# A two-layer SSD, window-attention and hyena encoder on one core: decay rows stored a second time, hyena forward transform by residues, key and value columns moved ahead

## The chip, the cores and the metric

The kernel runs on one core of one Trainium2 chip, in a single launch. The core's engines are TensorE (PE, matmuls, with PEld for its weight loads), VectorE (DVE), ScalarE (ACT), GpSimd (POOL) and SyncE (SP); each works through its own list of instructions in order and waits on semaphores for the others and for DMAs. The metric is the device time of one execution in microseconds (us), as the median of several runs. Lower is better.

## The reference

Two sequences (256 tokens "prompt", 512 tokens "sample") go with the same weights through two encoder layers of width 2048, all in float32. A layer is

```python
h = rms_norm(x, norm_g)
u = h @ w_in
z, xbc, dt_raw, q, k, v, g_att, hy_proj, g_hy = split(u)
y_ssd = ssd_branch(z, xbc, dt_raw, ...)      # width 1024
y_att = attention_branch(q, k, v, g_att, ...)  # width 512
y_hy = hyena_branch(hy_proj, g_hy, ...)      # width 512
x = x + concat([y_ssd, y_att, y_hy]) @ w_out
```

The state-space branch runs a scan in chunks of 128 tokens, forward and backward, for 16 heads of 64 channels: inside a chunk with a matrix of decays, and between chunks with a state that is multiplied into the output together with the exponent of the cumulative decay:

```python
lmat = exp(where(tril, a_cs[..., :, None] - a_cs[..., None, :], -inf))
y_diag = einsum('bcgels,bcsgep->bclgep', cb[:, :, :, None] * lmat, xdt)
y_off = einsum('bclgn,bcgepn,bcgel->bclgep', cm, prev, exp(a_cs))
```

The hyena branch multiplies spectra: `u = xb*v`, `y = irfft(rfft(u, 2L) * rfft(kern))[:L]`, `y = xa*(y + u*d)`. The attention looks at a window of 128 tokens to either side, with 8 query heads and 2 key/value heads. Each branch's output is multiplied by a SiLU gate and normalised.

## The kernel before

All 768 tokens (512 + 256, `T`) are held in channels-by-tokens layout. `OPH` and `OPL` are the high and low part of the layer's input operand in fp32r, a format in which a float32 product is made of three matmuls: high x high, high x low, low x high. The projection weights come in columns of 128 outputs, `W(0)` to `W(45)` per layer and then `w_out`. `gemm` (L141 is the matmul helper in the profile) computes one column: four loads of raw weights on SP's queue, eight splits of a weight tile (`split_w`: `hi` on ACT, then `lo` on DVE), and 16 k-tiles x 2 halves of the tokens x 3 products = 96 matmuls of 128x384 into the banks `gs` (tokens 0 to 383) and `gq` (384 to 767). One split serves 12 matmuls. The tiles of splits are few (a ring), so ACT may run only a little ahead of PE. All helpers that record an ACT, DVE or PE operation have the lines L138, L128/L135 and L141.

The order of the work is the program's own. Besides the columns there are generators, held by an object `Background`: after each quarter of a column `bg.step()` lets each of them run on to its next `yield`, so that its matmuls stand between those of the column, and its ACT and DVE work between splits. `bg.later(n, f)` runs `f` n steps later, `bg.mid` holds work that is run at the middle of the next quarter (`bg.half()`), and `bg.flush(g)` runs the rest of a generator at once. Generators' matmuls write PSUM tiles named `m` (four buffers); their SBUF tiles are `t` (pool `t2`, 16 buffers of 128x512) and `s` (pool `s3`, 14 buffers of 128x768).

In each layer the columns come in this order: W0 to W3 (the scan's B and C), the step sizes `dt` (`gemm_dt`), W4 to W11 (the scan's input, turned and stored in `XS(j)`), W12 to W19 (hyena's xb and v), W20 to W27 (the scan's gate z), W28 to W31 (hyena's xa), W32 (K), W33 (V), W34 to W37 (q), W38 to W41 and W42 to W45 (the gates of hyena and attention), then the 16 columns of `w_out`.

Three generators matter here.

- `ssd_gen` computes the cumulative decays `adt` summed along the chunk, turns them into rows, and stores them in DRAM as `rows_d` (L638). Then it works on eight pairs of heads (`pair`), each in some nine steps, with a new pair started while the last one is in its sixth. A pair loads its rows broadcast over the 128 partitions in three parts `R0`, `R1`, `R2` (`rows`, L684, two loads of 256 KB each), makes of each a decay matrix (`prep`: DVE subtracts, ACT takes Exp), then the chunk states, then the output of the states `Y`. For the last it needs the rows a second time in another layout, with head 0 on partitions 0 to 63 and head 1 on 64 to 127, four chunks in each direction: these are the decay rows `E2` (L726, four loads per pair). ACT takes their Exp (L750), DVE multiplies by `Y`. After the in-chunk matmuls (L758) come the six sums that write `XS(j)` (L760 to L767).

```python
src = rows_d[l, d, h0:h0 + 2, cs[i]:cs[i] + n, :]
load(out=t[:, i:i + n, :], in_=bass.AP(src.tensor, src.offset,
     [[NCH * 128, 2], [0, 64], [128, n], [1, 128]]))
```

- `hyena_gen` runs twice per layer (each for 256 channels, `hy[0]` and `hy[1]`). It turns its input into even and odd time points (`to_time`), and makes the forward transform by matmuls with a table (`forward`, L515): for the long sequence 24 matmuls of 128x256 at each of two calls, for 2 x 128 frequencies. `product` multiplies by the filter's spectrum; then the products and the inverse table are split into high and low part, and 48 inverse matmuls follow. The consumer of `W(28 + j)` flushes `hy[j // 2]` before it uses the result.
- `filter_gen` makes the filter spectra `kd` of the next layer with the same forward tables.

After the scan's gate the sum of squares goes through `rms`: PE's sums over partitions, ACT's square root, and `scale_ssd`, in which DVE scales the eight tiles of `XS` and POOL's queue stores them to `ys_d` (L1037). The attention's tiles then take the place of `XS`: `new_xs(F32R)` after the four `xa` columns gives out the same memory for K's high half `KH`, which the consumer of W32 writes with four ACT copies of 64x768 (L138, `XS<-s`), and for the queries. Every DMA but the weights' is issued on POOL's queue (a POOL instruction stands in line behind all before it); the weights' are on SP's.

Of the kernel before, what the change touches and what calls it, by code (L numbers as in the profile page):

```python
# [97 lines left out]
def trunk(ctx: ExitStack, tc: tile.TileContext, xT, w_in, w_dt, w_out, prm, brow, w1, mlpv, w2, w3, w4,  # L98
# [83 lines left out]
    rows_d = drp.tile([DEPTH, 2, 16, NCH, 128], F32, name="rows_d")  # L182
    ys_d = drp.tile([DEPTH, 8, 128, T], F32, name="ys_d")
# [215 lines left out]
    def filter_gen(l):  # L399
# [7 lines left out]
        for half in range(2):  # L407
            hc = slice(256 * half, 256 * half + 256)
            for pm in (1, 0):
# [40 lines left out]
                def freq_part(f, G, nk, L, slot):  # L450
# [11 lines left out]
                    if pm == 0:  # L462
                        STT(kk[:, 1], p[:, 0], 1.0 / L, kk[:, 1], MUL, SUB)
                    else:
                        STT(kk[:, 1], p[:, 0], -1.0 / L, kk[:, 1], MUL, ADD)
# [18 lines left out]
    def hyena_gen(l, half, us, ys):  # L484
# [9 lines left out]
        srcs = (((0, 256), (256, 512), (1, 256)), ((257, 512), (p0, p1), (p0 + 1, p1)))  # L494
        U = [[r3(), r3()] for _ in range(2)]

        def to_time(j):
            for b in range(2):
                p = mp((128, 3, 128))
                for i, (a, e) in enumerate(srcs[b]):  # L500
                    nc.tensor.transpose(p[:, i, :], us[j][:, a:e:2], ident)
                split(p, *(x[:, :, 128 * j:128 * j + 128] for x in U[b]))
# [12 lines left out]
        def forward(fs, ev, odd):  # L515
# [16 lines left out]
            TT(B[:, 1, :], cs[:, 1, :], pn[:, 0, :], SUB)  # L532
            return A, B

        def product(A, B, slot):
# [12 lines left out]
            TT(y[:, 0, :], B[:, 0, :], B[:, 1, :], SUB)  # L548
            TT(y[:, 1, :], B[:, 0, :], B[:, 1, :], ADD)
# [13 lines left out]
        AB = forward(fS, (0, 1), (2, 3))  # L563
        yield
        yield
# [38 lines left out]
    def ssd_gen(l, dtT, BT, CT, ready):  # L604
# [24 lines left out]
        yield  # L629
        for b in range(3):  # L630
# [25 lines left out]

        FW, BW = (0, 1, 2, 4), (1, 2, 3, 5)
# [16 lines left out]
        def pair(j, bt, cbF, cbB):  # L674
# [599 lines left out]
```

## Time and profile before

| | |
|---|---|
| median of 3 runs | 2487.45 us (2485.87 to 2487.83) |
| the profiled execution | 2489.0 us |
| its span in the trace | 2487.2 us |
| mean granted TensorE clock | 0.993 |
| PE busy | 2441.4 us, 98% |
| DVE, ACT, POOL busy | 64%, 44%, 14% |
| chain that ended last | PE 90%, DMA 4%, issue 2% |
| DMA | 266.22 MB, mean 107 GB/s |

The span runs from the first to the last instruction in the trace; the execution's own time is 1.8 us longer. "Busy" counts the time in which an engine has at least one instruction at work. A matmul's duration in the trace includes the time it overlaps its neighbours, so sums of durations on PE are larger than the time they take. The granted clock is the share of full speed that the chip gave TensorE in a stretch.

### The profile page before, as it was taken

The page shows a single profiled execution, that of the slowest core. Times are in us where ns is not written, and L with a number is a line of the kernel's source. Part 1 is how long each engine was busy: PE and PEld are TensorE (multiplying, and loading weights), DVE is VectorE, ACT ScalarE, POOL GpSimd, SP SyncE. Part 2 cuts the span into 40 slices and gives each one's busy share as a digit, 9 for nine tenths or more (in the row PEclk, how much of TensorE's full clock was granted, in tenths as well). Part 3 has the DMA queues.
Part 4 walks back from the last instruction along what each step waited for, and adds up shares of the span by engine and source line. Part 5 has one row for each costly group of instructions (what it writes and reads, how often), then busy time and mean ns, then how long its engine had stood idle before and what let it go on. Part 6 is the DMA issues. An engine that isn't in the chain of part 4 may idle for free.

```text
span 2487.2 us, 40924 instructions
## 1 busy us (share of the span) xinstructions
PE 2441.4 (98%) x15066; PEld 2393.2 (96%) x15066; DVE 1580.5 (64%) x3410; ACT 1087.5 (44%) x2560; POOL 341.4 (14%) x683
## 2 busy tenths in 40 slices
PE   8999999999999999999999999999999999999998
PEld 7999999999999999999999999999999999999997
DVE  6888775558856766544476787766746477573333
ACT  6467653334334444333353575633332355352332
POOL 2033221221100010121200332201001000000001
PEclk9999999999999999999999999999999999999999
DMA  4266542443421132344421555423213111332223
GB/s 169 63 153 146 142 129 86 129 133 124 140 78 60 51 100 80 112 149 132 146 96 55 141 149 149 135 85 106 94 60 128 63 54 47 106 109 89 77 82 132
DMA packets 126921, 266.22 MB, mean 107 GB/s; under 512 B 30175, under 2 KB 36666, under 8 KB 126720
## 3 DMA queue, kind: packets, MB, share of 16 engines
q1 hardware_dynamic: 78048, 136.35, 17.7%
q0 software_dynamic: 48672, 127.26, 17.2%
q8 instruction: 118, 1.93, 0.3%
q14 instruction: 83, 0.68, 0.1%
HBM read 231.23 MB, written 34.18 MB: 107 GB/s over the span
## 4 chain that ended last, share of the span: by engine, by line
PE 90%; DMA 4%; issue 2%; DVE 1%; ACT 1%; POOL 1%; DVEq 0%; ACTq 0%; POOLq 0%
PE gs L141 38%; PE gq L141 38%; PE m L141 12%; DMA t<-rows_d 3%; PE m L848 1%; PE gl L141 1%; POOL t L726 0%; ACT t L138 0%; DMA XS<-in_xT 0%; DMA s<-in_xT 0%; ACT hi L138 0%; DVE lo L128 0%; DVE t L135 0%; PE m L1000 0%; DVE t L128 0%
## 5 line engine op out<-in xcount | busy, mean ns | idle before, releaser
L138 ACT ACTIVATE hi<-raw 128x256 fp32r<-128x256 f32 x984 | 405.6, 414 | 1040.1 <-PE gq L141 920.5
L128 DVE TENSOR_TENSOR lo<-raw,hi 128x256 fp32r<-128x256 f32 x984 | 412.5, 421 | 597.9 <-ACT hi L138 587.0
L141 PE MATMUL gs<-OPH,hi 128*128 128x384 f32 x1920 | 657.4, 342 | 18.1 <-ACT OPH L138 11.0
L141 PE MATMUL gs<-OPH,lo 128*128 128x384 f32 x1920 | 645.0, 336 | 0.6 <-DVE lo L128 0.5
L141 PE MATMUL gq<-OPH,lo 128*128 128x384 f32 x1920 | 644.4, 336 | 0.0
L141 PE MATMUL gs<-OPL,hi 128*128 128x384 f32 x1920 | 644.0, 336 | 0.1
L141 PE MATMUL gq<-OPH,hi 128*128 128x384 f32 x1920 | 644.1, 335 | 0.0
L141 PE MATMUL gq<-OPL,hi 128*128 128x384 f32 x1920 | 643.3, 335 | 0.0
L141 PEld LDWEIGHTS gs<-OPH,hi 128*128 128x128 f32 x1920 | 362.4, 189 | 25.2 <-ACT OPH L138 11.3
L141 PEld LDWEIGHTS gs<-OPH,lo 128*128 128x128 f32 x1920 | 361.6, 188 | 2.7 <-DVE lo L128 2.7
L141 PEld LDWEIGHTS gs<-OPL,hi 128*128 128x128 f32 x1920 | 362.3, 189 | 0.8 <-DVE OPL L135 0.6
L141 PEld LDWEIGHTS gq<-OPH,hi 128*128 128x128 f32 x1920 | 361.8, 188 | 0.0
L141 PEld LDWEIGHTS gq<-OPL,hi 128*128 128x128 f32 x1920 | 361.6, 188 | 0.0
L141 PEld LDWEIGHTS gq<-OPH,lo 128*128 128x128 f32 x1920 | 361.5, 188 | 0.0
L128 DVE TENSOR_TENSOR t<-t,t 128x512 f32<-128x512 f32 (+3 forms) x260 | 169.1, 668 | 26.5 <-ACT t L138 23.6
L135 DVE SCALAR_TENSOR_TENSOR s<-cv,prm_t,s 128x770 f32<-128x770 f32 x144 | 145.9, 1015 | 22.6 <-ACT s L138 21.9
L138 ACT ACTIVATE t<-s,dt 128x128 f32<-128x128 f32 x384 | 133.6, 391 | 18.9 <-DVE t L135 18.5
L128 DVE TENSOR_TENSOR s<-s,s 128x768 f32<-128x768 f32 (+2 forms) x126 | 112.8, 904 | 27.3 <-ACT s L138 26.7
L138 ACT ACTIVATE t<-t 128x512 fp32r<-128x512 f32 (+3 forms) x132 | 77.3, 587 | 92.4 <-DMA t<-rows_d 48.6
L128 DVE TENSOR_TENSOR t<-m,t 128x256 f32<-128x256 f32 (+3 forms) x157 | 72.3, 485 | 18.3 <-PE m L141 5.8
L684 POOL DMA_DIRECT2D t<-rows_d x96 | 68.8, 719 | 103.9 <-DVE XS L128 38.0
L138 ACT ACTIVATE t<-t,acs 128x128 f32<-128x128 f32 x192 | 73.6, 389 | 13.6 <-DVE t L135 13.6
(225 smaller groups left out, 2572.6 us busy)
## 6 DMA issues: line engine op xcount, KB each, us to landing
raw<-in_w_in SPq DMA_DIRECT2D x368, 256.0 KB, 3.0
raw<-in_w_out SPq DMA_DIRECT2D x128, 256.0 KB, 3.0
t<-rows_d POOLq DMA_DIRECT2D x96, 256.0 KB, 6.4
s<-in_xT POOLq DMA_DIRECT2D x24, 384.0 KB, 4.4
xs_d<-s POOLq DMA_DIRECT2D x16, 385.0 KB, 4.2
s<-xs_d POOLq DMA_DIRECT2D x16, 385.0 KB, 9.3
t<-rows_d POOLq DMA_DIRECT2D x32, 192.0 KB, 10.5
t<-in_decay POOLq DMA_DIRECT2D x24, 256.0 KB, 4.9
```

The source lines that it names most:

```text
L128: (eng or nc.vector).tensor_tensor(out=o, in0=a, in1=b, op=op)
L135: (eng or nc.vector).scalar_tensor_tensor(out=o, in0=a, scalar=s, in1=b, op0=op0, op1=op1)
L138: nc.scalar.activation(o, i, f, **kw)
L141: nc.tensor.matmul(o, lhsT=l, rhs=r, start=start, stop=stop)
L684: load(out=t, in_=rows_d[l, d, h0:h0 + 2, 2 * u:2 * u + 2, :].partition_broadcast(128))
L848: nc.tensor.transpose(pt[g][:, 128 * kb:128 * kb + 128], s[g][:, 128 * kb:128 * kb + 128], ident)
```

## The change

Three things change, and some lines with them.

1. **A second copy of the decay rows.** `ssd_gen` stores the rows it turns, besides into `rows_d`, also into a new DRAM tensor `ed_d`, in which each head has the four chunks that `E2` wants side by side (six further small stores a layer). `E2` is loaded from there: four loads per pair as before, but each fills 64 partitions with 512 elements of one head. The six sums at a pair's end become a function that runs at the middle of the next quarter column.
2. **Residues.** The time points of the long sequence are taken in the order 0, 2, 1, 3 modulo 4 instead of even, odd, and the frequencies of the tables in an order that pairs each with its mirror. `residues` then makes two transforms of 12 matmuls each, whose sums and differences (`sets`) give all frequencies; the second load of the forward table goes. The inverse table is loaded by `iv_load`, a step or more ahead of its splits.
3. **K and V first.** W32 (K) and W33 (V) come before the four `xa` columns W28 to W31; `new_xs` moves into K's consumer.

```diff
+    ed_d = drp.tile([DEPTH, 2, 16, 4, 128], F32, name="ed_d")
...
-        srcs = (((0, 256), (256, 512), (1, 256)), ((257, 512), (p0, p1), (p0 + 1, p1)))
+        srcs = (((0, SL, 4), (2, SL, 4), (1, SL, 4)), ((3, SL, 4), (p0, p1, 2), (p0 + 1, p1, 2)))
...
+        def residues(fs, a, tts):
+            ps = [mp((128, 2, 256)) for _ in range(2)]
+            for p, (fh, fl), tt in zip(ps, fs, tts):
+                uh, ul = um(tt)
+                for c in range(2):
+                    for n, (x, y) in enumerate(((fh, uh), (fh, ul), (fl, uh))):
+                        MM(p[:, c, :], x[:, a + c, :], y, n == 0, n == 2)
+            s = t2((128, 2, 256))
+            nc.scalar.copy(out=s, in_=ps[1])
+            E, F = t2((128, 2, 256)), t2((128, 2, 256))
+            TT(E, ps[0], s, ADD)
+            TT(F, ps[0], s, SUB)
+            return E, F
+
+        def sets(E, G, turned):
+            A, B = t2((128, 2, 256)), t2((128, 2, 256))
+            if turned:
+                TT(A[:, 0], E[:, 0], G[:, 1], ADD)
...
+            else:
+                for o, c in ((A, 0), (B, 1)):
+                    TT(o[:, 0], E[:, c], G[:, c], ADD)
+                    TT(o[:, 1], E[:, c], G[:, c], SUB)
             return A, B
...
-        AB = forward(fS, (0, 1), (2, 3))
-        yield
+        E, F = residues(fS, 0, (0, 1))
+        yield
+        G, H = residues(fS, 2, (2, 3))
         yield
...
-        spec = [[split(x, r2(), r2()) for x in product(*AB, 0)]]
-        yield
-        fS = freq(fwS[1], 2)
-        yield
-        yield
-        AB = forward(fS, (0, 1), (2, 3))
-        yield
-        spec.append([split(x, r2(), r2()) for x in product(*AB, 1)])
-        pss = [mp((128, 2, 256)) for _ in range(2)]
-        for eo in range(2):
-            iv = []
+        def iv_load(eo):
+            g = []
             for i in range(2):
                 f = t2((128, 2, 256))
                 load(out=f, in_=ivS[i, :, 2 * eo:2 * eo + 2, :])
-                iv.append(split(f, r3()[:, 0:2], r3()[:, 0:2]))
+                g.append(f)
+            return g
+
+        spec = [[split(x, r2(), r2()) for x in product(*sets(E, G, False), 0)]]
+        g = iv_load(0)
+        yield
+        yield
+        spec.append([split(x, r2(), r2()) for x in product(*sets(F, H, True), 1)])
+        pss = [mp((128, 2, 256)) for _ in range(2)]
+        for eo in range(2):
+            iv = [split(f, r3()[:, 0:2], r3()[:, 0:2]) for f in g]
+            if eo == 0:
+                yield
+                g = iv_load(1)
             yield
             yield
...
+        FW, BW = (0, 1, 2, 4), (1, 2, 3, 5)
...
             for d in range(2):
-                load(out=rows_d[l, d, :, 2 * b:2 * b + 2, :],
-                     in_=r.rearrange("h (c d) t -> h d c t", d=2)[:, d])
+                v = r.rearrange("h (c d) t -> h d c t", d=2)[:, d]
+                load(out=rows_d[l, d, :, 2 * b:2 * b + 2, :], in_=v)
+                cs = [(i, c - 2 * b) for i, c in enumerate((BW, FW)[d]) if c // 2 == b]
+                i, c = cs[0]
+                load(out=ed_d[l, d, :, i:i + len(cs), :], in_=v[:, c:c + len(cs)])
...
-            for d, cs in ((0, BW), (1, FW)):
+            for d in range(2):
                 t = t2((128, 4, 128))
-                for i, n in ((0, 3), (3, 1)):
-                    src = rows_d[l, d, h0:h0 + 2, cs[i]:cs[i] + n, :]
-                    load(out=t[:, i:i + n, :], in_=bass.AP(src.tensor, src.offset,
-                         [[NCH * 128, 2], [0, 64], [128, n], [1, 128]]))
+                for hh in range(2):
+                    load(out=t[64 * hh:64 * hh + 64], in_=ed_d[l, d, h0 + hh].partition_broadcast(64))
                 E2.append(t)
...
-            yield
-            dsk = P(l, PDS, j)
...
+            def final():
+                dsk = P(l, PDS, j)
...
+            bg.mid.append(final)
             yield
...
-        for j in range(4):
-            def f(ps, pq):
-                bg.flush(hy[j // 2])
...
-        new_xs(F32R)
-        KH = [XS(6), XS(7)]
-        kL = s3p.tile([128, T], F32R, tag="s3", name="kL")
-        KL = [(kL[:, 0:SL], kL[:, SL:T]), (t2((128, SL), F32R), t2((128, PL), F32R))]
+        KH, KL = [], []
 
         def f(ps, pq):
+            new_xs(F32R)
+            KH.extend((XS(6), XS(7)))
+            kL = s3p.tile([128, T], F32R, tag="s3", name="kL")
+            KL.extend(((kL[:, 0:SL], kL[:, SL:T]), (t2((128, SL), F32R), t2((128, PL), F32R))))
...
         gemm_col(W(33), f)
+        for j in range(4):
+            def f(ps, pq):
+                bg.flush(hy[j // 2])
+                a = hconv(j, ps, pq)
...
+            gemm_col(W(28 + j), f)
```

The constant tables (`constants`) get the new order of time points and frequencies, and a few signs in `forward`, `product` and `filter_gen` follow from it; their sizes stay.

**How the instructions move.** On POOL's queue in layer 0, at the second pair of heads (`rows_d` are the stored rows, `t` the tiles they are loaded into, `xs_d` the scan's input stored by a column's consumer, `h_d` a store of the filter generator), before:

```order
L375 DMA h_d<-s_1643 128x768
L746 DMA s_1714<-xs_d 128x770
L684 DMA t_1832<-rows_d 128x2x256
L684 DMA t_1834<-rows_d 128x2x256
L684 DMA t_1915<-rows_d 128x2x256
L684 DMA t_1917<-rows_d 128x2x256
L726 DMA t_1919<-rows_d 128x1x384
L726 DMA t_1919<-rows_d 128x1x128
L726 DMA t_1922<-rows_d 128x1x384
L726 DMA t_1922<-rows_d 128x1x128
```

and with the change:

```order
L716 DMA t_1839<-rows_d 128x2x256
L776 DMA s_1721<-xs_d 128x770
L716 DMA t_1841<-rows_d 128x2x256
L716 DMA t_1922<-rows_d 128x2x256
L716 DMA t_1924<-rows_d 128x2x256
L757 DMA t_1926<-ed_d 64x512 x2
L757 DMA t_1929<-ed_d 64x512 x2
L118 MEMSET cv 128x2 x3
L376 DMA h_d<-s_1650 128x768
```

The four `E2` loads, each of 384 or 128 elements on 128 partitions, are now two and two of 512 on 64; the store of `h_d`, which stood ahead of the row loads, now follows them.

On ACT in layer 0, from the square roots of the scan's norm on (`hi<-raw` is a weight split, `r` hyena's splits of its turned input, `XS<-s` the write of K's high half), before:

```order
L138 ACT_TABLE_LOAD
L138 ACTIVATE s_6712<-m,eps_93 128x512
L138 ACTIVATE hi<-raw 128x256
L138 ACTIVATE s_6712<-m,eps_93 128x256
L138 ACTIVATE r_6900<-m 128x3x128
L138 ACTIVATE hi<-raw 128x256 x2
L138 ACTIVATE r_6900<-m 128x3x128
L138 ACTIVATE hi<-raw 128x256 x5
L138 ACTIVATE r_6902<-m 128x3x128 x2
L138 ACTIVATE hi<-raw 128x256
L138 ACTIVATE s_6929<-cv,prm_t 128x770
```

and with the change:

```order
L138 ACT_TABLE_LOAD
L138 ACTIVATE s_6715<-m,eps_93 128x512
L138 ACTIVATE s_6715<-m,eps_93 128x256
L138 ACTIVATE r_6809<-m 128x3x128 x2
L138 ACTIVATE hi<-raw 128x256 x7
L138 ACTIVATE r_6811<-m 128x3x128 x2
L138 ACTIVATE hi<-raw 128x256
L138 ACTIVATE XS<-s_6929 64x768 x3
L138 ACTIVATE hi<-raw 128x256
L138 ACTIVATE XS<-s_6929 64x768
```

The K writes now follow eight weight splits after the square roots, with a ninth split ahead of the last of the four; before, they stood in the column after the four `xa` columns, of which the last row here (`s` from `cv`) is the first one's convolution. By the built program the first K write waits for the stores to `ys_d`.

## Rows read from the trace of the kernel before

**Rows 1.** The page, busy time: engine, us, share of the span, instructions.

```profile
PE 2441.4 (98%) x15066; PEld 2393.2 (96%) x15066; DVE 1580.5 (64%) x3410; ACT 1087.5 (44%) x2560; POOL 341.4 (14%) x683
```

**Rows 2.** Stretches: window, length, busy us of PE PEld DVE ACT POOL, PEclk, DMA, GB/s.

```profile
187.40:193.40 6.00, 3.94 (x14) 3.37 (x13) 5.97 (x13) 6.00 (x20) 0.00 (x0) 0.72 0.13 44
271.40:282.40 11.00, 7.00 (x33) 6.73 (x32) 6.02 (x15) 5.53 (x14) 0.72 (x1) 0.69 0.28 83
353.40:355.60 2.20, 0.76 (x10) 0.43 (x6) 0.41 (x2) 1.37 (x4) 1.09 (x2) 1.00 0.13 28
690.70:701.90 11.20, 6.61 (x29) 5.99 (x29) 10.10 (x22) 5.25 (x9) 2.37 (x10) 0.70 0.26 75
1521.60:1531.60 10.00, 6.09 (x34) 5.82 (x33) 4.96 (x13) 4.45 (x11) 0.72 (x1) 0.83 0.27 80
1602.40:1609.90 7.50, 5.47 (x29) 5.07 (x26) 2.99 (x10) 5.77 (x19) 1.33 (x5) 0.77 0.40 121
...
2301.00:2363.00 62.00, 62.00 (x360) 62.00 (x359) 20.52 (x42) 19.24 (x38) 1.07 (x2) 1.00 0.24 77
```

**Rows 3.** PE's waits: waiting group, releaser, us in all, cases, longest.

```profile
PE m L141 <- DVE XS L135: 7.9, 2, 4.0
```

**Rows 4.** ACT's timeline, 325 to 356 us: start, us each, what, and its wait before.

```profile
328.95 0.64 ACT L138 ACTIVATE t<-t 128x512 f32<-128x512 f32 x1 [2.67 <-DMA t<-rows_d]
...
350.64 0.63 ACT L138 ACTIVATE t<-t 128x512 f32<-128x512 f32 x1 [4.22 <-DMA t<-rows_d]
...
354.23 0.63 ACT L138 ACTIVATE t<-t 128x512 f32<-128x512 f32 x1 [2.96 <-DMA t<-rows_d]
```

**Rows 5.** Line L726: its issues (ns min/median/max), who waits, the landings.

```profile
L726 POOL DMA_DIRECT2D t<-rows_d x64: 797/817/855, 132.7 to 1595.3; - x64
...
  ACT t L138: 48.6, 24
...
DMA to landing us min/median/max: 5.9/10.3/13.7
```

**Rows 6.** Line L684, the rows' loads: issue to landing.

```profile
DMA to landing us min/median/max: 3.5/6.4/8.4
```

**Rows 7.** DMA queues, 350 to 353 us, then 341 to 343 us.

```profile
q0 software_dynamic: 33, 0.12, 11.2%
...
q0 software_dynamic: 101, 0.33, 71.8%
```

**Rows 8.** PE's groups by form: busy us, mean ns, idle before.

```profile
L141 PE MATMUL m<-r,t 128*128 128x256 f32 x432 | 59.8, 291 | 4.6 <-ACT r L138 4.6
```

**Rows 9.** PE's timeline, 618 to 626 and 689 to 705 us.

```profile
619.57 5.59 PE L141 MATMUL m<-r,t 128*128 128x256 f32 x46
...
695.61 8.94 PE L141 MATMUL m<-r,t 128*128 128x256 f32 x48 [4.58 <-ACT r L138]
```

**Rows 10.** Line L412, loads of 64 rows of weights: issue and landing.

```profile
L412 POOL DMA_DIRECT2D t<-in_w x16: 528/539/559, 354.1 to 1203.5; - x16
...
DMA to landing us min/median/max: 2.1/2.7/9.8
```

**Rows 11.** POOL's timeline, 1365 to 1377 us.

```profile
1370.73 2.51 POOL L638 DMA_DIRECT2D rows_d<-t  x5 [0.92 <-issue]
...
1374.89 0.73 POOL L684 DMA_DIRECT2D t<-rows_d  x1 [0.92 <-DMA rows_d<-t]
```

**Rows 12.** DVE's timeline, 1376 to 1384 us.

```profile
1379.71 1.14 DVE L135 SCALAR_TENSOR_TENSOR t<-t,acs,t 128x128 f32<-128x128 f32 x4 [3.52 <-DMA t<-rows_d]
```

**Rows 13.** ACT's timeline, 628 to 632 us.

```profile
630.39 0.46 ACT L138 ACTIVATE s<-m,eps 128x256 f32<-128x256 f32 x1
```

**Rows 14.** POOL's timeline, 625 to 655 us.

```profile
646.05 0.54 POOL L1037 DMA_DIRECT2D ys_d<-XS  x1 [0.67 <-PE gq L141]
```

**Rows 15.** Line L1037, the stores of `ys_d`: issue to landing.

```profile
DMA to landing us min/median/max: 3.3/4.8/7.1
```

**Rows 16.** ACT's groups by form: busy us, mean ns, idle before.

```profile
L138 ACT ACTIVATE XS<-s 64x768 fp32r<-64x768 f32 x24 | 20.3, 844 | 3.9 <-DVE s L135 2.9 <-DVE s L128 0.7
```

More of the change, by code (lines that the diff above doesn't have):

```diff
@@ L499, in to_time @@
                 p = mp((128, 3, 128))
-                for i, (a, e) in enumerate(srcs[b]):
-                    nc.tensor.transpose(p[:, i, :], us[j][:, a:e:2], ident)
+                for i, (a, e, n) in enumerate(srcs[b]):
+                    nc.tensor.transpose(p[:, i, :], us[j][:, a:e:n], ident)
                 split(p, *(x[:, :, 128 * j:128 * j + 128] for x in U[b]))
@@ L531, in forward @@
             TT(B[:, 0, :], pn[:, 0, :], cs[:, 1, :], ADD)
-            TT(B[:, 1, :], cs[:, 1, :], pn[:, 0, :], SUB)
+            TT(B[:, 1, :], pn[:, 0, :], cs[:, 1, :], SUB)
+            return A, B
+        def residues(fs, a, tts):
[15 more added lines that the diff above has]
+                TT(A[:, 0], E[:, 0], G[:, 1], ADD)
+                TT(A[:, 1], E[:, 0], G[:, 1], SUB)
+                TT(B[:, 0], G[:, 0], E[:, 1], SUB)
+                STT(B[:, 1], G[:, 0], -1.0, E[:, 1], MUL, SUB)
+            else:
+                for o, c in ((A, 0), (B, 1)):
+                    TT(o[:, 0], E[:, c], G[:, c], ADD)
+                    TT(o[:, 1], E[:, c], G[:, c], SUB)
             return A, B
@@ L547, in product @@
             TT(x[:, 1, :], A[:, 0, :], A[:, 1, :], SUB)
-            TT(y[:, 0, :], B[:, 0, :], B[:, 1, :], SUB)
-            TT(y[:, 1, :], B[:, 0, :], B[:, 1, :], ADD)
+            TT(y[:, 0, :], B[:, 0, :], B[:, 1, :], ADD)
+            TT(y[:, 1, :], B[:, 0, :], B[:, 1, :], SUB)
             return x, y
@@ L655, in ssd_gen @@
         yield
-        FW, BW = (0, 1, 2, 4), (1, 2, 3, 5)
         def group(g):
@@ L758, in pair @@
                     MM(o, X[:, c, hh, :], Ms[c // 2][:, hh, c % 2, :])
-            yield
-            dsk = P(l, PDS, j)
-            yT = Xf.rearrange("p (c t) -> p c t", c=NCH)
-            STT(yT[:, 0:4], t[:, 0:SL].rearrange("p (c t) -> p c t", c=4), dsk, yS, MUL, ADD)
-            STT(yT[:, 4:6], t[:, SL + GAP:T + GAP].rearrange("p (c t) -> p c t", c=2), dsk, yP, MUL, ADD)
-            for d, cs in ((0, BW), (1, FW)):
-                for i, n in ((0, 3), (3, 1)):
-                    c = cs[i]
-                    TT(yT[:, c:c + n], yT[:, c:c + n], E2[d][:, i:i + n], ADD)
+            def final():
+                dsk = P(l, PDS, j)
+                yT = Xf.rearrange("p (c t) -> p c t", c=NCH)
+                STT(yT[:, 0:4], t[:, 0:SL].rearrange("p (c t) -> p c t", c=4), dsk, yS, MUL, ADD)
+                STT(yT[:, 4:6], t[:, SL + GAP:T + GAP].rearrange("p (c t) -> p c t", c=2), dsk, yP, MUL, ADD)
+                for d, cs in ((0, BW), (1, FW)):
+                    for i, n in ((0, 3), (3, 1)):
+                        c = cs[i]
+                        TT(yT[:, c:c + n], yT[:, c:c + n], E2[d][:, i:i + n], ADD)
+            bg.mid.append(final)
             yield
@@ L1077, in trunk @@
         gemm_col(W(33), f)
+        for j in range(4):
+            def f(ps, pq):
+                bg.flush(hy[j // 2])
+                a = hconv(j, ps, pq)
+                TT(yh[j][:, 0:SL], yh[j][:, 0:SL], a[:, 0:SL], MUL)
+                TT(yh[j][:, SL:T], yh[j][:, SL:T], a[:, SL + GAP:T + GAP], MUL)
+            gemm_col(W(28 + j), f)
         qs, QA = [], [[XS(2 * i % 6), XS(2 * i % 6 + 1)] for i in range(4)]
@@ L1174, in constants @@
     c = {}
-    order = {L: [np.arange(0, L, 2), np.arange(1, L, 2)] for L in (SL, PL)}
+    A = np.arange
+    order = {SL: [np.concatenate([A(e, SL, 4), A(e + 2, SL, 4)]) for e in range(2)],
+             PL: [A(e, PL, 2) for e in range(2)]}
     zs, decs = [], []
@@ L1192, in constants @@
         om = np.pi * (np.arange(h) + 0.5) / L
+        om[128:] = np.pi / 2 - om[:h - 128]
         fw = np.empty((h // 128, h // 128, 128, 4, 128), f)
```

10 lines of the change are left out of this document (2 added, 8 removed).

## The prediction

> **What bounds the kernel now.** I began with the busy times: PE 2441.4 of 2487.2 us [rows 1]. So whatever takes a matmul away, or an idle time of PE, counts in full, and ACT and DVE count only where PE ends up waiting for them. A quiet stretch gives the unit: 360 matmuls in 62.00 us without a gap [rows 2], 0.172 us each at 384 columns (their own durations overlap, so the spacing is the price).
>
> Next came PE's waits, and around each the table of stretches, which shows idle time and granted clock together. Five stretches lie in the state-space part: at 187, 271, 353, 1521 and 1602 us PE was busy 3.94 of 6.00, 7.00 of 11.00, 0.76 of 2.20, 6.09 of 10.00 and 5.47 of 7.50 us [rows 2]. That is 2.06+4.00+1.44+3.91+2.03 = 13.4 us idle. In four of the five the mean clock is below one (0.72, 0.69, 0.83, 0.77): after PE has stood still, the records show it for a while at the lower of its two levels, 1.2 instead of 2.4 GHz. Lost by that: 0.28x6 + 0.31x11 + 0.17x10 + 0.23x7.5 = 8.5 us. One more such place lies in layer 0's hyena: 690.7 to 701.9 us, busy 6.61 of 11.20 at 0.70, so 4.6 us idle and 3.4 us by the clock.
>
> Who is late in those five? After the program's first loads, PE's largest waits are for DVE's write of `XS` [rows 3], that is `final`'s sum. Before it stands ACT: at 350.64 and 354.23 us its Exp on the decay rows waited 4.22 and 2.96 us for the load from `rows_d` [rows 4], and the source line of these loads says 48.6 us of ACT waits in 24 cases [rows 5]. ACT's weight split stands behind that Exp, and PE behind the split. A wait of 2.67 us [rows 4] cost PE nothing visible; the 7.2 us pair cost it 1.44 us. So the cover is about 3 to 5 us.
>
> Why are these loads late? They land a median 10.3 us after issue (5.9 at least) [rows 5], the rows' loads of the pair itself, which are larger, after 6.4 [rows 6]. When practically only the decay rows are in flight, their queue keeps 11.2% of 16 engines busy, 1.8 engines; while the pair's own rows run, 71.8% [rows 7]. The old pattern has two heads as its outer dimension, and behaves as if two engines carry it. The Trainium skill, "DMA: Bandwidth & Descriptors", section "Rules for kernel authors", says that an outermost dimension smaller than 16 confines a DMA to that many engines; by that rule, the trace agrees (1.8 of 16).
>
> **The change part by part.** The sum is made against the profiled execution, 2489.0 us; the median of the runs, 2487.45, is 1.5 us less.
>
> *Residues.* The forward transforms of the long sequence go from 48 to 24 matmuls per generator, four generators: 96 of the 432 `m<-r,t` matmuls of 256 columns [rows 8]. 46 of them took 5.59 us back to back [rows 9], 0.118 us each when the last one's overlapping tail is taken off: 96 x 0.118 = **-11.3 us**. DVE and ACT lose eight loads' splits and gain some sums; they are not what PE waits for there, so nothing.
>
> *Decay rows loaded from `ed_d`.* Four loads per pair of 64 partitions, 2 KB a row, with 64 as the outermost dimension. No row of before has this shape. Issue: 539 ns for a 64-row load [rows 10] against 817 [rows 5], so the last one leaves 3x0.28 = 0.8 us sooner. Landing: at best like the 64-row load, 2.7 us [rows 10]; at worst unchanged, 10.3. I take 6.4 [rows 6], the landing of the pair's own rows: those share the stretch and the queue and are a broadcast too. Then the last rows are there about 4 to 5 us sooner. The pair of waits at 350 us falls from 7.2 to about 3 us, inside the cover. Of the 13.4 us idle I leave 1.5: **-11.9 us**, and the clock that fell behind it: **-8.5 us**. If nothing lands sooner both are zero.
>
> *The twelve small stores to `ed_d`,* six a layer, stand ahead of the first rows' loads on POOL's queue. Six at about 0.5 us (five took 2.51) is 3.0 us; the second of those loads already waited 0.92 us for a store [rows 11], so it moves by some 2 us. In layer 1 DVE waited 3.52 us for it [rows 12], so I take the delay as open: **+1.9 us**. In layer 0 the loads are used later and it is free. POOL's store of `h_d`, which had rows' loads queued behind it, now stands behind them; that only helps.
>
> *`final` half a step sooner:* the same instructions, buffers freed a little earlier; nothing.
>
> *K and V columns before the four `xa` columns.* The matmuls are the same. Gain: the flush of the second hyena moves two columns later. In the built order its last inverse matmul now stands 0.87 of a column ahead of the end of the column whose consumer flushes it. Before, 48 inverse matmuls ran in the open after PE had waited 4.58 us for their splits [rows 9]. So the place at 690 us goes: **-8.0 us** (4.6 idle, 3.4 clock). The inverse table's earlier load belongs here: its split no longer stands directly behind its load.
>
> Loss: K's high half is written over `XS`, and now has to wait until all eight `ys_d` stores land, which were four columns old before. In layer 0 of before, ACT's last square root began at 630.39 us and took 0.46 [rows 13]; the last store left at 646.05 [rows 14] and a store takes up to 7.1 us [rows 15]: 653.2. That is 22.3 us after the root. ACT reaches K's write eight weight splits after the root; each split serves 12 matmuls, 2.07 us, so after 16.6 us. It waits 5.7 us and then makes three writes of 0.84 us [rows 16] before the next split: 8.2 us. PE has two split tiles in hand (4.1 us) and, by the built order, 24 hyena matmuls there (2.8 us): **+1.3 us**. In layer 1 one more split stands ahead (18.6 us), the writes are interleaved with splits, and the wait stays under the 4.1 us: nothing. Behind these writes on ACT is only the split, and behind that PE.
>
> Sum: 2489.0 - 11.3 - 11.9 - 8.5 + 1.9 - 8.0 + 1.3 = 2452.5; as a median of runs **2451 us**.
>
> **The rivals.**
> 1. *K's write is not covered.* For it: the 8.2 us above stand against 6.9 of cover, and in layer 1 the same chain has less beside it. If PE idles 5 us in both layers and the clock falls each time as at 690 us (3.4): 2451 + 2x8.4 - 1.3 = 2466.
> 2. *Halves bring little.* Each new load fills half of the partitions. Priced as a whole 256 KB load each: the pair's own rows moved 0.33 MB in 2 us [rows 7], so such a load takes 1.6 us, and four in a row have landed 6.4 + 3x1.6 = 11.2 us after the first issue instead of 3x0.82 + 10.3 = 12.8. The five stalls shrink by 1.6 us each: 0.5+2.4+0+2.3+0.4 = 5.6 us stay instead of 1.5, with the clock of the two long ones, 3.4 + 1.7: 2451 + 4.1 + 5.1 = 2460. The Trainium skill, same page and section, speaks for that: it calls splitting one transfer into two partition halves useless, because they serialize. No run here shows it yet; by the rule the gain of this term would be that smaller one. Against it: the old loads used about two engines, so engines were to be had.
> 3. *The loads do not land sooner at all:* POOL's queue sets them, not the engines. The 11.2% [rows 7] speaks against it. 2451 + 11.9 + 8.5 = 2471.
> 4. *Slower: the buffers.* K's low half and V's tile hold two of 16 `t2` and two of 14 `s3` buffers four columns longer, in layer 0 while the second hyena runs and takes up to 16 `t2` itself. Each time ACT or DVE stands at a write without a buffer, splits stand behind it; one such place in the open cost 8.0 us (at 690 us). It ends slower from the sixth such place on, of some 14 steps of the second hyena: 2451 + 48 = 2499. Against it: PE's list of waits [rows 3] has no large entry for the hyena but the flush, with nearly as many buffers in use.
> 5. *Halved matmuls save less,* because PE is waiting in the hyena stretch anyway: half of 11.3, 2457. It lies within my range and has no chance of its own.
>
> **How the numbers follow.** Forecast 0.64 (its own range 2444 to 2458), K's write 0.11, halves 0.09, no sooner 0.06, slower by buffers 0.04. The last 0.06 is a better one: the small delays of ACT and DVE behind late rows, which leave no idle stretch of their own, shrink too; 2440. The range 2440 to 2470 leaves out cases 3 and 4 and some tail. A measurement of this kernel tells about 0.2%, 5 us, from no change. Every case but the buffers is more than that below 2487; with a mix of several losses in mind: faster 0.94, same 0.02, slower 0.04.
>
> **What would show it.** Right: the page's `m<-r,t` group has 336 matmuls; the new loads land in 4 to 7 us and ACT waits for them under 25 us in all; no half clock in the state-space stretches; no PE wait at the flush; mean clock above 0.996. Wrong: ACT's waits for the decay rows near 48 us (case 3), PE idle behind ACT's K write with a fall of the clock after it (case 1), ACT or DVE waits of several us in the columns between V and the flush (case 4).

## The result, and the profile after

The changed kernel takes **2446.75 us** (median of 4 runs, 2445.18 to 2448.84) against 2487.34 us before (median of 4, 2485.87 to 2487.83): a ratio of 0.9838, 95% interval 0.9821 to 0.9855. In the later run `after_again` below it took 2446.04 us, ratio 0.984 (0.9825 to 0.9855). Forecast were 2451 us, with a range of 2440 to 2470. One execution of the run `ed_two_heads` was granted a clock of 0.557 from end to end and took 4011 us; its trace is not used, and `ed_two_heads_b` is the same kernel again.

Of the page of the changed kernel, the busy times and the chain that ended last:

```profile
PE 2416.9 (99%) x14970; PEld 2371.5 (97%) x14970; DVE 1586.1 (65%) x3418; ACT 1082.9 (44%) x2544; POOL 323.7 (13%) x687
...
PE 92%; issue 4%; DMA 2%; POOL 1%; DVE 1%; ACT 1%; DVEq 0%; POOLq 0%; ACTq 0%
```

PE's busy time fell by 24.5 us [rows 1] and the span by 41.9 (2487.2 to 2445.3); the rest was idle time. The table of stretches at the same places of the work as in [rows 2] (columns as there): the five in the state-space part, then the hyena's end, and last a new place at 632 us.

```profile
185.10:190.50 5.40, 5.40 (x38) 5.40 (x38) 5.31 (x11) 4.22 (x11) 1.13 (x2) 1.00 0.15 52
262.40:270.70 8.30, 8.30 (x58) 8.27 (x57) 4.55 (x13) 4.04 (x9) 1.45 (x2) 1.00 0.47 150
340.00:343.00 3.00, 3.00 (x33) 2.58 (x32) 1.87 (x4) 1.87 (x7) 0.75 (x2) 1.00 0.26 87
672.00:684.70 12.70, 12.70 (x84) 12.26 (x84) 10.99 (x22) 6.31 (x11) 2.25 (x13) 1.00 0.36 109
1494.00:1500.00 6.00, 6.00 (x45) 5.96 (x44) 4.84 (x13) 3.98 (x11) 0.72 (x1) 1.00 0.37 109
1568.00:1574.10 6.10, 6.10 (x52) 5.68 (x51) 3.51 (x9) 3.07 (x11) 1.29 (x5) 1.00 0.42 143
632.50:638.50 6.00, 3.32 (x23) 3.03 (x22) 5.18 (x12) 3.09 (x7) 0.00 (x0) 1.00 0.13 44
```

All six old places are without a gap and at full clock. The one at 632 us is idle for 2.68 of 6 us, and the clock beside it stays 1.00. PE's group of hyena matmuls by form, and of its list of waits the row that belongs to 632 us:

```profile
L141 PE MATMUL m<-r,t 128*128 128x256 f32 x336 | 47.0, 284 | 3.6 <-DVE t L128 2.7 <-ACT t L138 0.9
...
PE m L141 <- DVE t L128: 2.7, 1, 2.7
```

336 matmuls instead of 432 [rows 8]. The source line of the new decay-row loads, with their issues, who waits, and the landings:

```profile
L757 POOL DMA_DIRECT2D t<-ed_d x64: 522/536/551, 132.3 to 1561.9; - x64
...
  ACT t L138: 3.1, 4
...
DMA to landing us min/median/max: 2.7/6.1/10.0
```

ACT's 48.6 us of waiting [rows 5] have become 3.1.

**Where the time went.** All kernels here issue the same projection matmuls (into `gs` and `gq`) in the same number, 11,648 of them in each trace. So the trace of each can be cut at the start of the same (counted) projection matmul, and the lengths of the pieces compared, whatever stands between. "Projection column" means 96 of them. The table gives the length before and the difference of each kernel's trace to it, in us; the pieces are named by what runs in them, with their time before. The start (to 65.7 us) varies by up to 1.6 us from run to run with the first loads, and so does not count.

| kernel (median us) | state space, layer 0: 65.7 to 391.5 | filters: to 544.3 | hyena, layer 0: to 760.6 | attention, output: to 1330.5 | state space, layer 1: to 1629.7 | hyena, layer 1: to 1982.6 | start and end | span |
|---|---|---|---|---|---|---|---|---|
| before (2487.3) | 325.8 | 152.8 | 216.3 | 570.0 | 299.2 | 352.8 | 570.4 | 2487.2 |
| changed (2446.75) | -13.4 | +0.1 | -12.5 | +1.1 | -10.9 | -5.8 | -0.5 | -41.9 |
| after_again (2446.0) | -13.7 | -0.2 | -12.5 | +0.1 | -10.9 | -5.8 | -1.6 | -44.6 |
| only_ed (2457.8) | -14.7 | -0.1 | -5.6 | +1.0 | -10.9 | -0.4 | -1.2 | -31.8 |
| only_residues (2471.3) | -1.1 | -0.1 | -11.7 | +1.0 | +0.1 | -5.6 | -1.1 | -18.5 |
| only_columns (2481.9) | +1.3 | +0.1 | -5.6 | +0.4 | -0.7 | +1.3 | -1.3 | -4.6 |
| after_old_loads (2472.6) | -4.5 | -0.2 | -11.0 | +0.2 | +2.0 | -5.8 | -1.5 | -20.7 |
| ed_two_heads_b (2478.1) | +2.9 | +0.4 | -9.5 | +0.1 | +1.5 | -5.8 | -0.6 | -11.0 |
| rows_halves (2451.3) | -8.9 | -0.1 | -13.4 | +1.4 | -10.9 | -5.8 | -0.3 | -37.9 |
| after_old_columns (2444.2) | -13.4 | 0.0 | -14.6 | +0.2 | -10.9 | -5.7 | -0.3 | -44.6 |
| v_first (2444.8) | -13.8 | -0.1 | -14.7 | +0.1 | -10.7 | -5.6 | -1.2 | -46.0 |
| old_columns_iv_late (2450.6) | -14.0 | +0.4 | -7.9 | +0.1 | -10.9 | -5.7 | -1.5 | -39.6 |
| tables_early (2443.9) | -13.0 | +0.7 | -15.3 | 0.0 | -10.8 | -5.7 | -1.4 | -45.5 |

Pieces in which PE never stands still repeat to about 0.4 us. Where it does, they differ by a microsecond or so between kernels that are alike there: `only_residues` and `only_columns` have the state space of before, and lie -1.1 to +1.3 us from it. From 409 us on the order of the matmuls changes in every kernel that has `final` half a step sooner (all but before, `only_residues` and `only_columns`), whatever its loads: a pair has a step less, and the generators behind the pairs run a step ahead. Twelve matmuls that ran behind 544.3 us then run ahead of it, and PE's waits around that cut shrink, in "filters" from 1.6 us to at most 0.8 and in the projection column behind it from 1.9 us to 0.4 to 1.2. In "filters" the added matmuls and the shorter waits cancel; the rest shows as a gain in "hyena, layer 0".

### The profile page after: what moved, and what is told of

Read it like the earlier page. It is cut to its first block, busy times and chain, and to the rows that moved or that the text cites. A ratio compares the mean times of both kernels' runs of the same rounds, so it can differ in the third digit from the quotient of the medians.

```text
span 2445.3 us, 40732 instructions
## 1 busy us (share of the span) xinstructions
PE 2416.9 (99%) x14970; PEld 2371.5 (97%) x14970; DVE 1586.1 (65%) x3418; ACT 1082.9 (44%) x2544; POOL 323.7 (13%) x687
## 2 busy tenths in 40 slices
DMA packets 113352, 264.01 MB, mean 108 GB/s; under 512 B 16799, under 2 KB 23418, under 8 KB 113152
## 4 chain that ended last, share of the span: by engine, by line
PE 92%; issue 4%; DMA 2%; POOL 1%; DVE 1%; ACT 1%; DVEq 0%; POOLq 0%; ACTq 0%
PE gs L141 39%; PE gq L141 39%; PE m L141 12%; PE m L879 1%; PE gl L141 1%; DMA t<-rows_d 1%; DMA t<-in_w 0%; PE m L1031 0%; DMA prm_t<-in_prm 0%; DMA t<-kd 0%; DMA t<-in_fwS 0%; ACT t L138 0%; DVE dt L135 0%; PE m L499 0%; POOL XS L1149 0%
## 5 line engine op out<-in xcount | busy, mean ns | idle before, releaser
L141 PE MATMUL gs<-OPH,hi 128*128 128x384 f32 x1920 | 655.2, 341 | 11.3 <-ACT OPH L138 10.7
L141 PEld LDWEIGHTS gs<-OPH,hi 128*128 128x128 f32 x1920 | 361.2, 188 | 16.8 <-ACT OPH L138 11.1
L128 DVE TENSOR_TENSOR t<-t,t 128x512 f32<-128x512 f32 (+4 forms) x280 | 174.3, 646 | 26.7 <-ACT t L138 24.5
L138 ACT ACTIVATE t<-s,dt 128x128 f32<-128x128 f32 x384 | 133.9, 391 | 14.0 <-DVE t L135 13.8
L138 ACT ACTIVATE t<-t 128x512 fp32r<-128x512 f32 (+2 forms) x124 | 71.4, 583 | 48.4 <-DVE t L128 27.4
L138 ACT ACTIVATE t<-t,acs 128x128 f32<-128x128 f32 x192 | 73.8, 389 | 11.3 <-DVE t L135 11.2
```

The costliest lines, as they stand in the source:

```text
L128: (eng or nc.vector).tensor_tensor(out=o, in0=a, in1=b, op=op)
L138: nc.scalar.activation(o, i, f, **kw)
L141: nc.tensor.matmul(o, lhsT=l, rhs=r, start=start, stop=stop)
```

## The experiments

**only_ed** is the kernel before with the first part of the change alone: the twelve stores to `ed_d`, the four loads, and `final`, as in the diff above.

> The kernel before with the second copy of the decay rows alone (its stores, the four 64-partition loads per pair, the six sums half a step later). My theory (terms add up, each in its own place): the stalls and the low clock of the state-space stretches go, and the columns' flush at 690 us and the 432 matmuls stay. The excess of PE over its usual spacing there fell by 24 us between the two traces, so 2463 us; by the forecast's terms (11.9 + 8.5 - 1.9) 2469. Rival: part of that gain came from the lighter load on DVE and ACT by the residues, or from the other order of columns; then this one gains less than 12 us, over 2475.

Measured: 2457.82 us, ratio 0.9888 (0.9873 to 0.9902). The state-space pieces gain 14.7 + 10.9 = 25.6 us, as much as in the changed kernel (24.3): the rival falls. A further 5.6 us came in layer 0's hyena, which no theory had expected: 2.4 in the projection column from 544 us on, where before PE waited three times for under 1 us each and where eight matmuls fewer stand now (this comes with `final`, see above), and 3.2 at the flush, where PE waits 2.83 us instead of 4.58 and less time passes at the lower clock (mean 0.86 from 674 to 686 us, so 1.7 us lost instead of 3.4).

**after_old_loads** is the changed kernel with the loads of before:

```diff
-                for hh in range(2):
-                    load(out=t[64 * hh:64 * hh + 64], in_=ed_d[l, d, h0 + hh].partition_broadcast(64))
+                for i, n in ((0, 3), (3, 1)):
+                    src = rows_d[l, d, h0:h0 + 2, cs[i]:cs[i] + n, :]
+                    load(out=t[:, i:i + n, :], in_=bass.AP(src.tensor, src.offset,
+                         [[NCH * 128, 2], [0, 64], [128, n], [1, 128]]))
```

> The changed kernel with the decay rows loaded from rows_d by the old pattern and without the twelve stores (the sums stay half a step later). My theory: the loads' landing alone makes the difference, so it loses the 20 to 24 us again: 2467 to 2471 us, ACT's waits for these loads near 48 us, and the clock low again behind two or more stalls. Rival (the sums' earlier place hides the late loads): under 2455.

Measured: 2472.58 us, ratio 0.9942 (0.9927 to 0.9957). Of the 24.3 us in the two state-space pieces 21.8 are lost again, although `final` stands where the change put it. The line of the loads:

```profile
  ACT t L138: 47.9, 23
...
DMA to landing us min/median/max: 5.9/10.5/13.2
```

The loads are what counts.

**ed_two_heads, ed_two_heads_b**: the second copy is stored and used, but each tile is filled by one load of 128 partitions with two heads as the outermost dimension.

```diff
-                for hh in range(2):
-                    load(out=t[64 * hh:64 * hh + 64], in_=ed_d[l, d, h0 + hh].partition_broadcast(64))
+                src = ed_d[l, d, h0:h0 + 2]
+                load(out=t, in_=bass.AP(src.tensor, src.offset, [[512, 2], [0, 64], [128, 4], [1, 128]]))
```

> The changed kernel with two loads per pair from ed_d instead of four: 128 partitions each, rows of 2 KB, two heads as the outermost dimension. My theory (the outermost dimension of 2 confines a load to about two engines): they land as late as the old ones, 10 us or more after issue, and the time goes back to 2460 to 2470 us. Rival (the old loads were slow for their rows of 512 and 1536 bytes, or for their longer issue): two loads with long rows are at least as fast as four, the time stays within 3 us of 2447.

> The same kernel as ed_two_heads, for a trace at full clock. By my theory the two loads land 10 us or more after issue in the stretches with row loads, near two of 16 engines are busy while only they are in flight, and the five stalls are back; its time was 2473 to 2488 us. Rival: they land like the four half loads (6 us) and something else made it slow.

Measured: 2480.67 us (median of nine), ratio 0.9974 (0.9961 to 0.9988), and 2478.08 us in the one execution of `ed_two_heads_b`. Fewer loads with longer rows, and the whole gain in the state-space part is gone. The line of the loads of `ed_two_heads_b`, then its DMA queue from 347 to 350 us, while only two of these loads are in flight; after that, in a fence of its own, the queue of the changed kernel from 332.8 to 334.2 us, while its four halves of the same pair are in flight.

```profile
L757 POOL DMA_DIRECT2D t<-ed_d x32: 817/828/852, 132.2 to 1590.4; - x32
...
  ACT t L138: 48.6, 16
...
DMA to landing us min/median/max: 7.3/11.2/14.2
...
q0 software_dynamic: 77, 0.27, 24.7%
```

```profile
q0 software_dynamic: 98, 0.29, 71.2%
```

24.7% of 16 engines are 4.0 for two loads, so about two each; 71.2% are 11.4. That is the outermost dimension at work, with rows of 2 KB in both. It comes with a second difference, which I had not looked for: many more small packets. The pages of `after_old_loads`, of the changed kernel and of `ed_two_heads_b`, which differ in the stores of the rows and in these loads alone, count them:

```profile
DMA packets 126280, 264.11 MB, mean 107 GB/s; under 512 B 30047, under 2 KB 36538, under 8 KB 126080
...
DMA packets 113352, 264.01 MB, mean 108 GB/s; under 512 B 16799, under 2 KB 23418, under 8 KB 113152
...
DMA packets 127175, 264.11 MB, mean 107 GB/s; under 512 B 30623, under 2 KB 37242, under 8 KB 126976
```

In `ed_two_heads_b` they come first: from 345 to 347 us 848 of the queue's 866 packets are under 512 B, and 0.08 MB is all it moves. So some of the 7 to 14 us until such a load lands may be the small packets' time, and not the few engines'; no run parts the two, and both go with the two heads outermost. At this place the first of the two loads was issued at 343.75 us and landed for ACT at 351.65, after 7.9 us; the four halves of the changed kernel were issued from 331.56 us on, and ACT stood for them 0.76 us (POOL's and ACT's timelines, `ed_two_heads_b` first).

```profile
343.75 0.83 POOL L757 DMA_DIRECT2D t<-ed_d  x1 [2.63 <-PE m L141]
...
351.65 0.63 ACT L138 ACTIVATE t<-t 128x512 f32<-128x512 f32 x1 [5.51 <-DMA t<-ed_d]
```

```profile
331.56 2.11 POOL L757 DMA_DIRECT2D t<-ed_d  x4 [2.56 <-PE m L141]
...
335.34 0.63 ACT L138 ACTIVATE t<-t 128x512 f32<-128x512 f32 x1 [0.76 <-DMA t<-ed_d]
```

**rows_halves** does without the second copy: each tile is filled from `rows_d` by four loads of 64 partitions.

```diff
-                    load(out=t[64 * hh:64 * hh + 64], in_=ed_d[l, d, h0 + hh].partition_broadcast(64))
+                    for i, n in ((0, 3), (3, 1)):
+                        load(out=t[64 * hh:64 * hh + 64, i:i + n, :],
+                             in_=rows_d[l, d, h0 + hh, cs[i]:cs[i] + n, :].partition_broadcast(64))
```

> The changed kernel without the second copy: eight loads per pair from rows_d, each for the 64 partitions of one head, of three chunks or one. My theory: 64 as the outermost dimension is what helps, so they land nearly as early; the issue takes 8 x 0.54 = 4.3 us instead of 2.1, so the last lands some 2 us later than from ed_d: 2447 to 2455 us. Rival (rows of 2 KB are what helps): near the old loads, 2465 to 2471 us.

Measured: 2451.31 us, ratio 0.9857 (0.9841 to 0.9874), as my theory had it. So the copy is not what helps; the halves are. What it costs to do without it lies in layer 0's state space alone (-8.9 against -13.4 us). The line of the loads: they land early, but POOL, with twice as many of them, stood 27 times until an earlier load from `rows_d` had landed. The trace's semaphores show that the program itself asks for this: POOL's DMAs take eight semaphores in turn, and none leaves before the one eight places ahead of it has landed (the loads at 136.69, 137.65, 139.21 and 140.43 us each left 0.28 us after that).

```profile
  DMA t<-rows_d: 26.4, 27
...
  ACT t L138: 7.1, 5
...
DMA to landing us min/median/max: 2.3/4.1/8.4
```

**only_columns** is the kernel before with W32 and W33 ahead of W28 to W31 (third part of the change), **after_old_columns** the changed kernel with them behind again.

> The kernel before with K and V ahead of the xa columns alone. My theory: -8.0 us at the flush and +1.3 to +2.9 us behind K's write: 2480 to 2482 us, with no low clock near 690 us. Rival: without the residues and the earlier table the second hyena ends later, so the flush still waits: 2485 us or more.

> The changed kernel with W32 and W33 behind the four xa columns again. My theory: K's write no longer waits (the 2.9 us of PE behind it go), and the flush of the second hyena stands in the open again (4.6 us idle and 3.4 us of low clock): 2447 - 2.9 + 8.0 = 2452 us. Rival: the earlier load of the inverse table is what took the wait at the flush away, and the order of the columns only costs; then 2444 us.

Measured: 2481.88 us, ratio 0.9983 (0.9974 to 0.9993), and **2444.17 us**, ratio 0.9826 (0.9809 to 0.9842). Alone the move gains 5.6 us in layer 0's hyena, about as expected, and loses 1.3 us in layer 1's, which was not. On top of the rest it costs: with the old order that piece is 2.1 us shorter, no wait at the flush comes back, and all four runs (2443.66 to 2444.40) lie below all eight of the changed kernel (2444.46 to 2448.84), which were taken in other runs; the piece of the changed kernel is the same in both its traces (-12.5). The rival was right about the time; what took the wait away, `old_columns_iv_late` shows. PE's timeline at the end of the second hyena in `after_old_columns`, where before 48 matmuls ran after a wait of 4.58 us [rows 9]:

```profile
658.28 0.50 PE L141 MATMUL m<-r,t 128*128 128x256 f32 x2
659.15 1.36 PE L141 MATMUL m<-r,t 128*128 128x256 f32 x10
...
671.77 2.96 PE L141 MATMUL m<-r,t 128*128 128x256 f32 x22
```

They come in pieces now, the first twelve 13 us ahead of the last, with no wait.

**v_first**: in the changed kernel the blocks of W33 (V) and W32 (K) change places; no line in them differs.

> The changed kernel with V (W33) ahead of K (W32), so that K's write comes a column later (16.6 us) after the stores to ys_d. My theory: in the changed kernel ACT's first write of K waits 4.27 us for these stores and PE 2.9 us behind it; a column later they have landed, and 2.9 us go: 2444 us. Rival: PE's wait there comes from the DVE work of K's two low parts (eight sums of 0.5 us ahead of the forward transform's sums) rather than from the stores; then it goes with K into the next column and the time stays at 2447 us.

Measured: 2444.81 us, ratio 0.9828 (0.9813 to 0.9842). The hyena piece of layer 0 is 2.2 us shorter (-14.7 against -12.5) and PE's list no longer has the wait of 2.7 us. It has a smaller one instead:

```profile
PE m L141 <- DVE r L128: 0.7, 1, 0.7
```

This one ends at 657.22 us, in the column behind K's, where K's last four low sums (2.07 us from 652.70 us on) stand in DVE's list ahead of the splits that PE waits for. So my theory holds for 2.2 of the 2.9 us, and the rest looks like the rival's DVE work, which did go with K; that was not tried apart.

**only_residues** is the kernel before with the second part of the change: residues and `iv_load`.

> The kernel before with the residues and the earlier table load alone (old decay-row loads, old order of columns). My theory after the last runs: 96 matmuls less (-11.3 us) and no wait at the flush in spite of the old order (-8.0 us): 2468 us. Rival: the flush's wait goes only where the decay rows are early too, since the state-space part then ends sooner; then 2476 us, with an idle time of PE near 690 us.

Measured: 2471.27 us, ratio 0.9939 (0.9924 to 0.9953). The hyena piece of layer 1, which had no stall, loses 5.6 us: half of 11.3. That of layer 0 loses 11.7, so 6.1 more (8.0 by my theory; PE now waits 1.15 us at 606.78 us, in the first hyena), in the old order of columns. The rival's wait near 690 us did not show.

**old_columns_iv_late** loads the inverse table in the old place.

```diff
-        g = iv_load(0)
...
-            iv = [split(f, r3()[:, 0:2], r3()[:, 0:2]) for f in g]
+            g = iv_load(eo)
+            iv = [split(f, r3()[:, 0:2], r3()[:, 0:2]) for f in g]
             if eo == 0:
                 yield
-                g = iv_load(1)
```

> The kernel after_old_columns with the inverse table loaded again directly ahead of its splits. Theory A (the earlier table load took the flush's wait away): the wait of 3 to 5 us and the low clock behind it are back, 2449 to 2452 us. Theory B (the shorter forward transform did, it leaves the second hyena fewer matmuls and one table less to wait for): within 1.5 us of 2444.

Measured: 2450.6 us, ratio 0.9859 (0.9842 to 0.9875): theory A's time, but not its place. PE's timeline and the stretch around it:

```profile
590.75 5.82 PE L141 MATMUL m<-r,t 128*128 128x256 f32 x24 [5.43 <-ACT r L138]
...
584.90:596.00 11.10, 5.58 (x25) 4.97 (x24) 9.82 (x19) 3.98 (x7) 2.27 (x5) 0.71 0.41 118
```

This is the first hyena's inverse, where before had no wait; the second one's flush stayed quiet. Of the kernels in the old order those with the shorter transform have no wait at the second flush, with the earlier table (`only_residues`, `after_old_columns`) or without it (this one), and those with the long transform have it (before, `only_ed`). So the second hyena's wait went by the shorter transform (nine steps instead of ten from the long transform on; a step is a quarter column, 24 matmuls of 0.172 us, 4.1 us and more with what stands between), and the edit of the earlier table is what keeps the first hyena's matmuls from standing in one block behind the table's split. The built order of the matmuls differs between the two kernels, and I cannot part the order's share from the load's.

**tables_early** adds to `after_old_columns` an earlier load of the forward tables (loads and splits in functions of their own: the long table's load is a step earlier, the short table's splits are a step later); **after_again** is the changed kernel beside it.

> The kernel after_old_columns with the forward tables loaded a step ahead of their splits. My theory: ACT's wait of 1.49 us for the table load and PE's 1.31 us behind it at 549 us go, all else stays: 2443 us, against 2447 of the changed kernel on the same chip. Rival: the tables' tiles are held a step longer and a t2 buffer is missing elsewhere: 2444 us or more.

> The changed kernel itself, on the same chip as tables_early: 2447 us by every theory. It is there for the comparison: tables_early should be 3 to 4 us faster.

Measured: 2443.88 us, ratio 0.9832 (0.9817 to 0.9846), against 2446.04 us. A gain of 2.2 us over the changed kernel, in the median of the runs, but none over `after_old_columns` that can be told: ACT still waited 1.07 us for the table at 549 us, and its load was issued at 544.95 us, against 544.75 in `after_old_columns`, so in the built order it had not moved. PE's wait behind it was 1.15 us in `after_old_columns` and 0.70 here; the 1.31 us of my theory is ACT's own wait for DVE just ahead of the table's.

## Why the prediction was right, step by step

*Residues, -11.3 us*: right. In layer 1's hyena, where nothing else changed, the changed kernel gains 5.8 us and the residues alone 5.6; twice that is 11.1 to 11.6.

*Decay rows from `ed_d`, with the stores, -11.9 - 8.5 + 1.9 = -18.5 us*: the mechanism is right, and the size was too small by 5.8 us, since the two pieces gained 24.3. The landing I took, 6.4 us, measured 6.1; two engines for the old loads are shown by `ed_two_heads_b`. The Trainium skill, "DMA: Bandwidth & Descriptors", section "Rules for kernel authors", says that an outermost dimension under 16 confines a DMA to at most that many engines. This trace agrees, with 4.0 engines for two loads of two heads each. What was mis-sized:
- The 1.5 us of idle that I left in the five places are not there. The five projection columns that hold them are together 22.5 us shorter (3.9, 7.3, 1.9, 5.8, 3.5), against 21.9 counted for idle time and clock. With the 1.3 us below that is 23.8 of the 24.3.
- "+1.9 us" for the stores is the term that had the wrong sign. POOL's and DVE's timelines of the changed kernel in layer 1:

```profile
1344.19 0.54 POOL L670 DMA_DIRECT2D rows_d<-t  x1 [39.53 <-ACT t L667]
...
1349.70 0.51 POOL L673 DMA_DIRECT2D ed_d<-t  x1
1350.20 1.45 POOL L716 DMA_DIRECT2D t<-rows_d  x2
...
1355.73 0.35 DVE L135 SCALAR_TENSOR_TENSOR t<-t,acs,t 128x128 f32<-128x128 f32 x1 [1.14 <-DMA t<-rows_d]
```

The stores do hold up the first rows: DVE takes them up 11.5 us after the first store began, against 10.4 before (the store ahead of those in [rows 11] began at 1369.27 us; DVE in [rows 12]). But DVE waits 1.14 us instead of 3.52, since in its list two sums of the convolution and a weight split now stand ahead of the rows' work, which before stood behind it. These two columns became 1.3 us shorter. I had read the stores' effect from the order on POOL's queue and had not looked at DVE's.

*K and V first, -8.0 + 1.3 us*: the sum for layer 0's hyena came out (5.65 of residues and 6.7 make 12.4; measured 12.5), but its parts are others. That it agrees is luck. The step that failed is "So the place at 690 us goes" as a gain of the columns: with the residues in the kernel that place is quiet in either order. `only_residues` takes 6.1 us there, `only_columns` 5.6 in that piece, `only_ed` 3.2 at the flush; one stall is mended twice over, and by a third edit in part, and it pays once. The column from 544 us on, which I had not counted, is 2.3 us shorter in the changed kernel, and that is `final`'s doing, not the loads': with the old loads and the new `final` it is 2.2 us shorter (`after_old_loads`), with the new order of columns or the residues and the old `final` 0.0 (`only_columns`, `only_residues`). And the move costs 2.1 us on top of the others: -6.1 - 2.3 + 2.1 = -6.3, against a measured -6.8 beside the matmuls.

*K's write*: the chain was followed rightly as far as ACT. The last root ended at 609.05 us and the last store was issued at 624.13; with the 6.05 us that the trace gives to its landing that is 630.18, 21.1 us after the root (forecast 22.3). ACT's write began at 630.51 after 4.27 us (forecast 5.7). The view puts it down to the filter loads behind the stores, but those landed at 631.13 and 631.61, after the write had begun. ACT's, DVE's and PE's timelines:

```profile
608.00 1.05 ACT L138 ACTIVATE s<-m,eps 128x512 f32<-128x512 f32 x2
...
624.13 0.54 POOL L1068 DMA_DIRECT2D ys_d<-XS  x1 [0.66 <-DVE XS L128]
...
630.51 2.57 ACT L138 ACTIVATE XS<-s 64x768 fp32r<-64x768 f32 x3 [4.27 <-DMA t<-kd]
...
634.01 2.07 DVE L128 TENSOR_TENSOR t<-s,XS 64x512 fp32r<-64x512 f32 x4
636.46 1.41 DVE L128 TENSOR_TENSOR t<-m,t 128x256 f32<-128x256 f32 x4
...
637.35 1.65 PE L141 MATMUL m<-r,t 128*128 128x256 f32 x12 [2.68 <-DVE t L128]
```

PE lost 2.68 us, not 1.3. "Behind these writes on ACT is only the split, and behind that PE" left out DVE: K's low parts wait for the write, and behind them in DVE's list stand the sums that free a PSUM tile for the next forward matmuls. In layer 1 nothing was lost, as forecast.

*The rivals.* K's write (2466): in layer 0 alone, and without a fall of the clock. Halves (2460): for the four halves issued from 331.56 us on ACT waited 0.76 us, and 11.4 engines were at work on them. The Trainium skill, same page and section, advises against two transfers to disjoint partition halves. Where the single transfer has an outermost dimension of two these traces differ: the halves landed after 2.7 us at the least and 6.1 in the median, the single loads after 7.3 and 11.2. No sooner (2471): ACT's waits of 3.1 us exclude it. Buffers (2499): no such place in the list of waits; `after_old_columns` bounds the whole cost of the move at 2.1 us, K's wait in it. The better tail (2440) is what happened in part.

*What stays open:* `final` half a step sooner was not tried alone. I had put it at nothing; it is worth 2.3 us behind the state space, by the paragraph above. In the state-space pieces `after_old_loads` keeps 2.5 us, little more than kernels that are alike there differ by; with the early loads no run shows what it is worth there. Nor did any run have the few engines without the small packets.

**The better version.** `after_old_columns`, at 2444.17 us, lies below both kernels; `v_first` and `tables_early` cannot be told from it. Its gain over the changed kernel is some 2 us, 0.1%, which the runs alone could hardly tell; the pieces of the traces can (PE idle for 1.5 us of layer 0's hyena, against 3.7 in both traces of the changed kernel).

## What to carry to other kernels

When a small load is late, ask how many engines carry it: the busy share of its queue while it is alone in flight gives the number, and splitting it so that each piece has partitions outermost may be worth more than making its rows longer. When one stall can be mended in several ways, try them apart before you add their gains: here each of three edits took away all or part of the same wait, and one of them, the other order of columns, then only brought a new one. And follow a wait through every engine that takes part in it: a late write on ACT reached PE through DVE's list, not through the split behind it.

## What the runs showed of the hardware that was not expected

- An idle time of PE and the fall of the clock do not go together in size. Around 187 us 2.06 us of idle time came with a mean clock of 0.72 [rows 2], around 632 us in the changed kernel 2.68 us with 1.00.
- A load of 128 partitions in one piece, with two heads as its outermost dimension, landed later than the same bytes in two pieces of 64 (medians 11.2 and 6.1 us), with the same source rows.
- The kernels with two heads outermost in these loads have some 13,000 to 14,000 more packets under 512 B (30,047 and 30,623 against 16,799), though their rows are 512 B and longer.
